# Attention of a hybrid layer: the score matmuls of two heads in two stretches per pair instead of four, the value matmuls in front of the first of them, 32 slots for every pair

## The chip, the core and the metric

The kernel runs on one core of a Trainium2 chip. Times are device microseconds of one execution. The kernel before was timed three times: 844.68, 844.88 and 845.14 us, median 844.88. The profile is of one further execution, which took 844.63 us; its span, from the first to the last instruction, is 842.8 us.

The engines are named as the profile names them: PE does the matmuls (PEld is its loading of the stationary operand), DVE is the vector engine, ACT the scalar engine, POOL the general engine, SP a queue that only issues transfers.

## What is computed

One decoder layer on 512 tokens of width 2048:

```
h = rms_norm(x);  z = h @ w_in                       # 2048 x 7168
a_val, a_glu, a_gate, q, k, v, b_gate = split(z)     # 1024 columns each
u = causal_depthwise_conv(a_val * sigmoid(a_glu))    # 31 taps
u = silu(layer_norm(u));  y_a = (u @ pw + b) * silu(a_gate)
q, k = rms_norm per head (16 heads of 64)
o = dilated_attention_mixture(q, k, v)               # causal, three window patterns
y_b = o * silu(b_gate)
out = x + concat(y_a, y_b) @ w_out
```

The three patterns of the attention are one softmax over all 512 keys, with the logarithm of the number of patterns that hold a key as a bias: a table (`tab`) that has -1e30 where none does.

## The kernel before, in words

**Units and slots.** All large matrix products are written as 76 units, each of 4 x 128 rows of a weight matrix by 512 columns. A unit is eight slots, and in a slot PE gets six matmuls of 512 columns (a product of two 16-bit halves, three matmuls each: `tri`, L360; the first 8 units use `exact_matmuls`, L713, in another number format). The loop at L810 counts the slots in `clock[0]`. Before a slot's matmuls it runs what a calendar holds for this slot (`after(n, fn)` puts `fn` n slots ahead), then the unit's own extras: in slot 0 of a unit ACT makes the high half `wh` of the next unit's weights (`split_hi`), in slot 2 DVE makes the low half `wl` (`split_lo`). PE needs both when the next unit begins. An instruction's place in the queue of its engine is thus set by the slot in which it was written; each engine works off its own queue in order and waits on semaphores for what other engines make.

**What fills DVE.** The depthwise convolution is a chain of DVE operations, written by a generator (`conv`, L476). `run_conv` (L702) takes one or more steps of it per slot, as long as the work given to DVE so far, counted in elements, is below 1200 per slot. After the last tap the generator writes the LayerNorm: sums over the eight channel tiles, a matmul with ones for the mean (L502), squares, a second set of matmuls for the variance (`token_rsqrt`, L342), the normalised tiles and `u16`, which the units named `pw` need from slot 448 on.

**Attention.** The heads go in eight pairs, four after the k projections of each half. `attention` (L647) starts pairs 32 slots apart in the first half and 40 in the second (`PERIOD`), always at the first slot of a unit. Within a pair (`two_heads`, L567) the plan at L636 says how many slots after the start each step is written:

- `scores(i)` for query tile i (128 queries, 128(i+1) keys): six matmuls with 64 rows of the array each, the two heads in the two row halves, then one DVE operation per head that adds `tab`, moves the scores to `sx` and takes the row maximum. Tiles 0, 1, 2, 3 stand at slots 0, 1, 4 and 5.
- `shift`, `exps` (ACT), `roots`, `high` and `low` (DVE; `high` on ACT in the first half) make normalised probabilities in two 16-bit halves, and `turn` transposes them by a DMA.
- `values`: 60 matmuls of 128 columns with 64 columns of the array each, the two heads in the two column halves, three slots before the next pair starts. `put` then multiplies with the gate on DVE, or copies on ACT where the gate isn't there yet.

PSUM has eight banks: four for the large products (`lin_ps`), three (`s_ps`) in turn for scores and small sums, one (`o_ps`) for `values`. A matmul that opens a bank waits until what the bank held has been read.

Of the kernel before, what the change touches and what calls it, by code (L numbers as in the profile page):

```python
# [10 lines left out]
F32 = mybir.dt.float32  # L11
# [5 lines left out]
OP = mybir.AluOpType  # L17
AX = mybir.AxisListType

P = 128  # L20
S = 512
# [10 lines left out]
LP = 4  # L32
WARM = 9
KU = 4
PERIOD = {0: 32, 1: 40}
START = 180
NORM_FROM = 37
PACE = 1200
# [37 lines left out]
def layer(ctx: ExitStack, tc: tile.TileContext, xt, w1, w2, w3, g_in, conv_w, conv_b,  # L76
          ln_g, ln_b, pw_b, q_g, k_g, table, out):
    nc = tc.nc
    A, G, T = nc.scalar, nc.gpsimd, nc.tensor
    V = Weighed(nc.vector)  # L80
    pool = lambda name, bufs, **kw: ctx.enter_context(tc.tile_pool(name=name, bufs=bufs, **kw))
    PS = bass.MemoryType.PSUM
# [6 lines left out]
    wide = pool("wide", 8)  # L89
    att = pool("att", 4)  # L90
    lin_ps = pool("lin_ps", LP, space=PS)
    s_ps = pool("s_ps", 7 - LP, space=PS)
    o_ps = pool("o_ps", 1, space=PS)
    ctx.enter_context(tc.manual_schedule())

    def slot(name):
# [13 lines left out]
    clock = [-1]  # L110

    def after(n, fn):

        calendar.setdefault(clock[0] + max(n, 1), []).append(fn)
# [361 lines left out]
    def conv():  # L476

        for i0 in range(0, 8, 2):
            while i0 + 1 not in u:
                yield 1  # L480
            for i in (i0, i0 + 1):
                cv[i] = slot("cv")
                A.activation(cv[i], u[i], AF.Identity, scale=cw[:, i, TAPS - 1:TAPS], bias=cb[:, i:i + 1])
            yield 2
            for j in range(TAPS - 2, -1, -1):
                d = TAPS - 1 - j
                for i in (i0, i0 + 1):
                    V.scalar_tensor_tensor(cv[i][:, d:], u[i][:, :S - d], cw[:, i, j:j + 1], cv[i][:, d:],
                                           op0=OP.mult, op1=OP.add)
                    yield 0  # L490
            u.pop(i0), u.pop(i0 + 1)

        wait[1] = True
        acc = temp("lnacc")
        V.tensor_add(acc, cv[0], cv[1])
        yield 0
        for i in range(2, 8):
            V.tensor_add(acc, acc, cv[i])
            yield 1
        yield 3  # L500
        mean = s_ps.tile([P, S], F32, name="ps_s")
        T.matmul(mean, ones, acc, start=True, stop=True)  # L502
        yield 1
        mean_sb = temp("mean")
        A.activation(mean_sb, mean, AF.Copy, scale=1.0 / C)
        yield 2
        acc2 = slot("lnacc2")
        squares = []
        for i in range(8):
            V.tensor_sub(cv[i], cv[i], mean_sb)  # L510
            if len(squares) > 1:
                V.tensor_add(acc2, acc2, squares.pop(0))
            if i == 0:
                A.activation(acc2, cv[i], AF.Square)
            else:
                squares.append(temp("lnsq"))
                A.activation(squares[-1], cv[i], AF.Square)
            yield 1 + i % 2
        while squares:
            yield 1  # L520
            V.tensor_add(acc2, acc2, squares.pop(0))
        yield 4
        c = small.tile([P, NT], F32, name="lncol")
        row = temp("lnrow")
        for _ in token_rsqrt(acc2, C, LN_EPS, c, row):
            yield 2
        yield 2
        for i in range(8 + 2):
            if i < 8:
                V.tensor_mul(cv[i], cv[i], row)  # L530
            if 1 <= i < 8 + 1:
                A.activation(cv[i - 1], cv[i - 1], AF.Silu, scale=lng[:, i - 1:i], bias=lnb[:, i - 1:i])
            yield 2
            if i >= 2:
                u16[i - 2] = split16(cv.pop(i - 2), scales["u"][0], "u16")
            yield 1
# [30 lines left out]
    def two_heads(pair):  # L567


        hf, p4 = divmod(pair, 4)  # L570
        halves = (slice(0, DH), slice(DH, P))
        st = [small.tile([P, 4 * NT], F32, name=f"st{a}") for a in range(2)]
        top, neg, total, root = ([t[:, j * NT:(j + 1) * NT] for t in st] for j in range(4))
        x = [att.tile([P, ALL], F32, name="sx", tag="att") for _ in range(2)]
        got = {}

        def scores(i):
            w = WIDTH[i]
            ps = [s_ps.tile([P, S], F32, name="ps_s") for _ in range(2)]
            for n, (q, k) in enumerate(((0, 0), (0, 1), (1, 0))):  # L580
                for a, rows in enumerate(halves):
                    T.matmul(ps[a][:, :w], qs[hf, q][rows, p4, i * P:w], ks[hf, k][rows, p4, :w], start=n == 0, stop=n == 2)  # L582
            for a in range(2):
                V.tensor_tensor_reduce(x[a][:, FROM[i]:FROM[i] + w], ps[a][:, :w], tab[:, S - w:], scale=1.0, scalar=-3e38,
                                       op0=OP.add, op1=OP.max, accum_out=top[a][:, i:i + 1])

        def shift(a):
            V.tensor_scalar(neg[a], top[a], nsc, None, op0=OP.mult)

        def exps(a, i):  # L590
            xi = x[a][:, FROM[i]:FROM[i] + WIDTH[i]]
            A.activation(xi, xi, AF.Exp, scale=sc, bias=neg[a][:, i:i + 1], accum_out=total[a][:, i:i + 1])  # L592

        def roots(a):
            V.tensor_scalar(total[a], total[a], 2.0 ** -P_SHIFT, None, op0=OP.mult)
            V.reciprocal(root[a], total[a])

        def high(a, i):
            if i == 0:
                got["p", a] = att.tile([P, 2 * ALL], F16, name="hl", tag="att")  # L600
            xi = x[a][:, FROM[i]:FROM[i] + WIDTH[i]]
            hi, r = got["p", a][:, FROM[i]:FROM[i] + WIDTH[i]], root[a][:, i:i + 1]
            if hf == 0:
                A.activation(hi, xi, AF.Copy, scale=r)
            else:
                V.tensor_scalar(hi, xi, r, None, op0=OP.mult)

        def low(a, i):
            hi, lo = (got["p", a][:, f + FROM[i]:f + FROM[i] + WIDTH[i]] for f in (0, ALL))
            V.scalar_tensor_tensor(lo, x[a][:, FROM[i]:FROM[i] + WIDTH[i]], root[a][:, i:i + 1], hi,  # L610
                                   op0=OP.mult, op1=OP.subtract)

        def turn(a):
            got["t", a] = att.tile([P, 2 * ALL // P, P], F16, name="pt", tag="att")
            nc.sync.dma_start(got["t", a], got["p", a], transpose=True)

        def values():
            got["o"] = po = o_ps.tile([P, S], F32, name="ps_o")
            for i in range(NT):
                for j in range(i + 1):  # L620
                    for n, (vp, pp) in enumerate(((0, 0), (1, 0), (0, 1))):
                        for a, rows in enumerate(halves):
                            T.matmul(po[rows, i * P:(i + 1) * P],  # L623
                                     vs[hf][j // 2][:, j % 2, 2 * p4 + a, vp * DH:(vp + 1) * DH],
                                     got["t", a][:, pp * (ALL // P) + FROM[i] // P + j, :],
                                     start=j == n == 0, stop=j == i and n == 2)

        def put():
            if pair in bg:
                ob[pair] = got["o"]  # L630
            else:
                ob[pair] = slot("opair")
                A.activation(ob[pair], got["o"], AF.Copy)
            gate_o(pair)

        plan = [(n, lambda i=i: scores(i)) for n, i in ((0, 0), (1, 1), (4, 2), (5, 3))]  # L636
        for a, e, h in ((0, 6, 10), (1, 14, 18)):
            plan += [(6 + a, lambda a=a: shift(a)), (h - 1, lambda a=a: roots(a)), (h + 6 - a, lambda a=a: turn(a))]
            for i in range(NT):
                plan += [(e, lambda a=a, i=i: exps(a, i)), (h + i // 2, lambda a=a, i=i: high(a, i)),  # L640
                         (h + 3 + i // 2, lambda a=a, i=i: low(a, i))]
        plan += [(PERIOD[hf] - 3, values), (PERIOD[hf] - 2, put)]
        return plan

    at_head = {}

    def attention(hf):  # L647
        start = -(-max(clock[0] + 28, max(at_head.values(), default=0) + PERIOD[0]) // 8) * 8
        for p4 in range(4):
            at_head[4 * hf + p4] = start + p4 * PERIOD[hf]  # L650

            def begin(pair=4 * hf + p4):
                for n, fn in two_heads(pair):
                    if n == 0:
                        fn()
                    else:
                        after(n, fn)
            after(at_head[4 * hf + p4] - clock[0], begin)


    def evac(group, m, ps):
# [228 lines left out]
```

## Time and profile before

| | |
|---|---|
| three timed runs, us | 844.68, 844.88, 845.14 |
| profiled execution, us | 844.63 |
| its span, us | 842.8 |
| PE busy, share of the span | 99% |
| DVE busy | 73% |
| ACT busy | 55% |
| POOL busy | 12% |
| granted TensorE clock | 1.00 |

The profile gives for each engine its instructions with start and length, and for each idle time what ended it. PE's matmuls overlap each other, so their lengths say less than the distance from one start to the next. The chain of waits lists the work that ended last, piece by piece, and so shows PE's stretches by such distances. Times in it are from the start of the span.

### The profile page before, as it was taken

Reading aid. Unit: us, or ns where it says so; the run is one execution under the profiler, and the core shown is the slowest. Engines: PE = TensorE matmul, PEld = TensorE weight load, DVE = VectorE, ACT = ScalarE, POOL = GpSimd, SP = SyncE. Lnnn points to the kernel's source line nnn. Section 1 sums busy time; section 2 is a strip of 40 time slices with the busy share of each in tenths; the row PEclk is TensorE's granted clock in tenths of the full one; section 3 lists DMA queues with packets and bytes.
Section 4 is the critical chain, followed back from the end, with each engine's and each line's share of the span. In section 5 each row is a group of like instructions: output and inputs, shape, how many; then the busy total and the mean of one; then the engine's idle time right before and its main releaser. Section 6 shows DMA issues by size and latency. Waiting matters only on the chain.

```text
span 842.8 us, 11262 instructions
## 1 busy us (share of the span) xinstructions
PE 838.2 (99%) x4394; PEld 413.3 (49%) x4394; DVE 611.5 (73%) x1023; ACT 462.6 (55%) x603; POOL 101.0 (12%) x131
## 2 busy tenths in 40 slices
PE   9999999999999999999999999999999999999998
PEld 6887644444444444444444444444444444444444
DVE  6658989888888978697878789286347697634343
ACT  7676644353655456676747558577486563333110
POOL 0001010101413101013031110001000000111100
PEclk9999999999999999999999999999999999999999
DMA  9922332222343525344555716326234476221022
GB/s 345 335 92 100 116 134 100 100 100 101 119 131 119 131 100 142 104 116 127 157 144 138 175 53 159 103 87 175 100 82 131 163 214 187 100 100 51 1 100 100
DMA packets 78948, 108.15 MB, mean 128 GB/s; under 512 B 62000, under 2 KB 62384, under 8 KB 69680
## 3 DMA queue, kind: packets, MB, share of 16 engines
q1 hardware_dynamic: 78608, 107.38, 41.5%
q8 instruction: 34, 0.56, 0.3%
q14 instruction: 18, 0.15, 0.1%
q10 hardware_dynamic: 288, 0.07, 0.0%
HBM read 88.56 MB, written 4.19 MB: 110 GB/s over the span
## 4 chain that ended last, share of the span: by engine, by line
PE 98%; DVE 1%; DMA 0%; issue 0%; ACT 0%; SPq 0%; DVEq 0%; ACTq 0%
PE ps_l L362 28%; PE ps_l L364 28%; PE ps_l L363 28%; PE ps_l L727 11%; PE ps_s L582 2%; PE ps_o L623 2%; DMA x<-xt_dram 0%; DVE wl L71 0%; PE ps_s L356 0%; PE ps_s L346 0%; DVE ya L71 0%; PE ps_s L502 0%; ACT hh L318 0%; DVE sx L71 0%; SPq L255 0%
## 5 line engine op out<-in xcount | busy, mean ns | idle before, releaser
L286 ACT ACTIVATE wh<-wf,ws 128x2048 f16<-128x2048 f32 x68 | 135.9, 1998 | 202.0 <-PE ps_l L363 195.8
L71 DVE SCALAR_TENSOR_TENSOR wl<-wf,ws,wh 128x2048 f16<-128x2048 f32 x68 | 159.7, 2348 | 37.1 <-ACT wh L286 36.8
L71 DVE SCALAR_TENSOR_TENSOR cv<-u,cw,cv 128x511 f32<-128x511 f32 (+14 forms) x240 | 161.6, 728 | 0.0
L362 PE MATMUL ps_l<-x,wh 128*128 128x512 f16 x384 | 145.7, 379 | 0.0
L362 PE MATMUL ps_l<-wh,x 128*128 128x512 f16 x384 | 145.7, 379 | 0.0
L364 PE MATMUL ps_l<-wh,x 128*128 128x512 f16 x384 | 145.5, 379 | 0.0
L363 PE MATMUL ps_l<-wl,x 128*128 128x512 f16 x384 | 145.5, 379 | 0.0
L364 PE MATMUL ps_l<-x,wl 128*128 128x512 f16 x384 | 145.5, 379 | 0.0
L363 PE MATMUL ps_l<-x,wh 128*128 128x512 f16 x384 | 145.5, 379 | 0.0
L182 ACT ACTIVATE junk<-wf 128x2048 bf16<-128x2048 f32 x68 | 129.1, 1898 | 3.5 <-DMA wf<-w_dram 3.4
L362 PEld LDWEIGHTS <-wh 128*128 128x128 f16 x708 | 69.2, 98 | 86.0 <-issue 5.5
L364 PEld LDWEIGHTS <-wl 128*128 128x128 f16 x708 | 69.2, 98 | 83.3 <-DVE wl L71 0.5
L363 PEld LDWEIGHTS <-wh 128*128 128x128 f16 x708 | 69.2, 98 | 77.8 <-issue 0.7
L363 PE MATMUL ps_l<-y,wh 128*128 128x512 f16 (+1 forms) x260 | 97.5, 376 | 0.0
L362 PE MATMUL ps_l<-y,wh 128*128 128x512 f16 (+1 forms) x260 | 97.5, 376 | 0.0
L364 PE MATMUL ps_l<-y,wl 128*128 128x512 f16 (+1 forms) x260 | 97.5, 376 | 0.0
L71 DVE SCALAR_TENSOR_TENSOR res<-ps_l,esc,res 128x512 f32<-128x512 f32 (+2 forms) x49 | 36.0, 737 | 53.7 <-PE ps_l L364 48.9
L196 POOL TENSOR_SCALAR ws<-ws 128x1 f32<-128x1 f32 x26 | 9.7, 372 | 520.8 <-DVE ws L71 520.8
L362 PEld LDWEIGHTS <-x 128*128 128x128 f16 x384 | 37.5, 98 | 47.1 <-issue 2.9
L364 PEld LDWEIGHTS <-x 128*128 128x128 f16 x384 | 37.5, 98 | 45.3
L363 PEld LDWEIGHTS <-x 128*128 128x128 f16 x384 | 37.5, 98 | 42.8
L592 ACT ACTIVATE sx<-sx,st,sc 128x128 f32<-128x128 f32 (+1 forms) x64 | 41.0, 641 | 28.1 <-DVE st L71 28.0
(179 smaller groups left out, 903.8 us busy)
## 6 DMA issues: line engine op xcount, KB each, us to landing
wf<-w_dram SPq DMA_DIRECT2D x72, 1024.0 KB, 4.9
x<-xt_dram SPq DMA_DIRECT2D x16, 256.0 KB, 6.6
res<-xt_dram SPq DMA_DIRECT2D x16, 256.0 KB, 5.4
out_dram<-res SPq DMA_DIRECT2D x15, 256.0 KB, 2.0
wf<-w_dram SPq DMA_DIRECT2D x7, 512.0 KB, 7.2
wf<-w_dram SPq DMA_DIRECT2D x2, 256.0 KB, 3.5
tab<-table_dram SPq DMA_DIRECT2D x1, 256.0 KB, 3.5
q<-qhl SPq DMA_TRANSPOSE x16, 3.2
```

The lines of the kernel that those rows point to most:

```text
L71: return getattr(self.engine, name)(out, src, *args, **kw)
L182: A.activation(junk[:, :n], src, AF.Square, scale=scale, accum_out=acc)
L196: G.tensor_scalar(scale, scale, 1e-30, 2.0 ** (-2 * top), op0=OP.max, op1=OP.mult)
L286: A.activation(parts[i][0], raw[i], AF.Copy, scale=wscale[units[i][3:]][0])
L362: T.matmul(ps, ah, bh, start=first, stop=False)
L363: T.matmul(ps, ah, bl, start=False, stop=False)
L364: T.matmul(ps, al, bh, start=False, stop=last)
L582: T.matmul(ps[a][:, :w], qs[hf, q][rows, p4, i * P:w], ks[hf, k][rows, p4, :w], start=n == 0, stop=n == 2)
L592: A.activation(xi, xi, AF.Exp, scale=sc, bias=neg[a][:, i:i + 1], accum_out=total[a][:, i:i + 1])
L623: T.matmul(po[rows, i * P:(i + 1) * P], vs[hf][j // 2][:, j % 2, 2 * p4 + a, vp * DH:(vp + 1) * DH], got["t", a][:, pp * (ALL // P) + FROM ...
L727: T.matmul(banks[group, m], wt[:, a, m * P:(m + 1) * P], xk[b], start=k == 0 and a == b == 0, stop=k == KC - 1 and a == 1)
```

## The change

Four things change. The scores of a pair are written in two stretches: tile 3 alone at the pair's first slot, then tiles 0, 2 and 1 three slots later, with tiles 0 and 2 of a head side by side in one bank. `values` and `put` of a pair are written where the next pair begins, directly in front of its first scores (for the last pair, one period after its start). The bank of `o_ps` joins `s_ps`, which has four banks now. Every pair has 32 slots and starts at the third slot of a unit; the steps between get other slots. In the LayerNorm two waits are added: the mean's matmul goes to the first slot of a unit, the variance's matmuls to the fifth slot of a unit in which no pair has begun within 8 slots.

```
-PERIOD = {0: 32, 1: 40}
+PERIOD = {0: 32, 1: 32}
+PHASE = 2
-    s_ps = pool("s_ps", 7 - LP, space=PS)
-    o_ps = pool("o_ps", 1, space=PS)
+    s_ps = pool("s_ps", 8 - LP, space=PS)
...
         yield 3
+        while clock[0] % 8:
+            yield 1
         mean = s_ps.tile([P, S], F32, name="ps_s")
...
         yield 4
+        while clock[0] % 8 != 4 or (clock[0] - at_pair[4]) % PERIOD[1] < 8:
+            yield 1
...
-        def scores(i):
-            w = WIDTH[i]
-            ps = [s_ps.tile([P, S], F32, name="ps_s") for _ in range(2)]
-            for n, (q, k) in enumerate(((0, 0), (0, 1), (1, 0))):
...
+        def scores(tiles):
+
+            ps = {}
+            for group in tiles:
+                for a in range(2):
+                    bank = s_ps.tile([P, S], F32, name="ps_s")
+                    for n, i in enumerate(group):
+                        f = sum(WIDTH[j] for j in group[:n])
+                        ps[i, a] = bank[:, f:f + WIDTH[i]]
+            order = [i for group in tiles for i in group]
+            for i in order:
+                w = WIDTH[i]
+                for n, (q, k) in enumerate(((0, 0), (0, 1), (1, 0))):
+                    for a, rows in enumerate(halves):
+                        T.matmul(ps[i, a], qs[hf, q][rows, p4, i * P:w], ks[hf, k][rows, p4, :w], start=n == 0, stop=n == 2)
+            for i in order:
+                w = WIDTH[i]
+                for a in range(2):
+                    V.tensor_tensor_reduce(x[a][:, FROM[i]:FROM[i] + w], ps[i, a], tab[:, S - w:], scale=1.0, scalar=-3e38,
+                                           op0=OP.add, op1=OP.max, accum_out=top[a][:, i:i + 1])
...
-            got["o"] = po = o_ps.tile([P, S], F32, name="ps_o")
+            got["o"] = po = s_ps.tile([P, S], F32, name="ps_o", tag="ps_s")
...
-        plan = [(n, lambda i=i: scores(i)) for n, i in ((0, 0), (1, 1), (4, 2), (5, 3))]
+        plan = [(0, lambda: scores(((3,),))), (3, lambda: scores(((0, 2), (1,))))]
...
-        plan += [(PERIOD[hf] - 3, values), (PERIOD[hf] - 2, put)]
...
+    def end_pair(pair):
+
+        for fn in to_come.pop(pair, ()):
+            fn()
...
-        start = -(-max(clock[0] + 28, max(at_head.values(), default=0) + PERIOD[0]) // 8) * 8
+        start = max(clock[0] + 28, max(at_pair.values(), default=0) + PERIOD[0])
+        start += (PHASE - start) % 8
...
-                for n, fn in two_heads(pair):
+                end_pair(pair - 1)
+                plan, values, put = two_heads(pair)
+                to_come[pair] = values, put
+                for n, fn in plan:
...
+                after(PERIOD[hf], lambda: end_pair(pair))
```

By the slot numbers that the loop counts, the eight pairs start at 224, 256, 288, 320, 352, 392, 432 and 472 before, and at 226, 258, ..., 450 (32 apart throughout) after the change; `values` of the last pair stand at 509 before and 482 after. The mean's matmul stands at 359 before and 360 after, the variance's at 380 and 396, the last `u16` tile at 415 and 431.

PE's queue, where the values of the first pair end. Before (`ps_o` is the values' bank, `pt` the transposed probabilities, `ps_l` a bank of the large products):

```order
L623 LDWEIGHTS v_2422
L623 MATMUL ps_o<-pt,v_2422 64x128
L362 LDWEIGHTS wh
L362 MATMUL ps_l<-x_978,wh 128x512
L363 LDWEIGHTS wh
L363 MATMUL ps_l<-x_978,wh 128x512
```

With the change (`ps_s` is a bank of scores):

```order
L638 LDWEIGHTS v_2419
L638 MATMUL ps_o<-pt,v_2419 64x128
L595 LDWEIGHTS q_1867
L595 MATMUL ps_s<-k_2189,q_1867 128x512
L595 LDWEIGHTS q_1867
L595 MATMUL ps_s<-k_2189,q_1867 128x512
L595 LDWEIGHTS q_1867
L595 MATMUL ps_s<-k_2191,q_1867 128x512
```

What followed the last value matmul was a matmul on the whole array; now it is the next pair's first score matmul on half of the rows.

DVE's queue at the second pair's scores. Before (`sx` takes the scores of one head, the rows `ISA st` with one column are the row maximum that goes with it, `cv` is the convolution):

```order
L71 ISA sx,st_2893<-ps_s,tab 128x256
L71 ISA st_2893 128x1
L71 ISA sx,st_2894<-ps_s,tab 128x256
L71 ISA st_2894 128x1
L71 SCALAR_TENSOR_TENSOR cv<-u,cw,cv 128x507
L71 SCALAR_TENSOR_TENSOR wl<-wf,ws,wh 128x2048
L71 ISA sx,st_2893<-ps_s,tab 128x384
L71 ISA st_2893 128x1
L71 ISA sx,st_2894<-ps_s,tab 128x384
L71 ISA st_2894 128x1
L71 ISA sx,st_2893<-ps_s,tab 128x512
```

With the change:

```order
L72 SCALAR_TENSOR_TENSOR gate<-ps_o,osc,gate 128x512
L72 ISA sx,st_2910<-ps_s,tab 128x512
L72 ISA st_2910 128x1
L72 ISA sx,st_2911<-ps_s,tab 128x512
L72 ISA st_2911 128x1
L72 SCALAR_TENSOR_TENSOR wl<-wf,ws,wh 128x2048
L72 ISA sx,st_2910<-ps_s,tab 128x128
L72 ISA st_2910 128x1
L72 ISA sx,st_2911<-ps_s,tab 128x128
L72 ISA st_2911 128x1
L72 ISA sx,st_2910<-ps_s,tab 128x384
```

The reads of tile 3's scores now stand in front of the low half `wl` of the next weights, and those of tiles 0, 2 and 1 behind it, one after the other; before, `wl` stood between the reads of tile 1 and those of tile 2.

DVE's queue in the units of slots 488 and 496, where `y` are the gated results made 16-bit for the last products (`ag` and `yas` for the convolution's, `yb1s` for the second half of the heads), up to the `wl` that the unit of slot 504 needs. Before:

```order
L71 SCALAR_TENSOR_TENSOR res<-ps_l,esc,res 128x512
L71 SCALAR_TENSOR_TENSOR hl<-sx,st_5738,hl 128x384
L71 SCALAR_TENSOR_TENSOR hl<-sx,st_5738,hl 128x512
L71 SCALAR_TENSOR_TENSOR y_6045<-ag_4590,yas,y_6045 128x512
L71 TENSOR_SCALAR y_6068<-gate,yas 128x512
L71 SCALAR_TENSOR_TENSOR res<-ps_l,esc,res 128x512
L71 SCALAR_TENSOR_TENSOR y_6068<-gate,yas,y_6068 128x512
L71 TENSOR_SCALAR y_6092<-gate,yas 128x512
L71 TENSOR_REDUCE ws<-ps_s 128x1
L71 SCALAR_TENSOR_TENSOR res<-ps_l,esc,res 128x512
L71 SCALAR_TENSOR_TENSOR y_6092<-gate,yas,y_6092 128x512
L71 SCALAR_TENSOR_TENSOR wl<-wf,ws,wh 128x2048
```

With the change:

```order
L72 SCALAR_TENSOR_TENSOR y_6108<-ag_4568,yas,y_6108 128x512
L72 SCALAR_TENSOR_TENSOR y_6110<-gate,yb1s,y_6110 128x512
L72 TENSOR_SCALAR y_6130<-gate,yas 128x512
L72 TENSOR_SCALAR y_6132<-gate,yb1s 128x512
L72 SCALAR_TENSOR_TENSOR res<-ps_l,esc,res 128x512
L72 SCALAR_TENSOR_TENSOR y_6130<-gate,yas,y_6130 128x512
L72 SCALAR_TENSOR_TENSOR y_6132<-gate,yb1s,y_6132 128x512
L72 TENSOR_SCALAR y_6157<-gate,yas 128x512
L72 TENSOR_REDUCE ws<-ps_s 128x1
L72 SCALAR_TENSOR_TENSOR res<-ps_l,esc,res 128x512
L72 SCALAR_TENSOR_TENSOR y_6157<-gate,yas,y_6157 128x512
L72 SCALAR_TENSOR_TENSOR wl<-wf,ws,wh 128x2048
```

The last pair's `hl` operations have left this stretch, and four of the `y` of `yb1s`, two operations each, have come into it, in front of the second `wl`.

## Rows read from the trace of the kernel before

**Rows 1.** The page: busy time of engines, granted clock in 40 slices.

```profile
PE 838.2 (99%) x4394; PEld 413.3 (49%) x4394; DVE 611.5 (73%) x1023; ACT 462.6 (55%) x603; POOL 101.0 (12%) x131
...
PEclk9999999999999999999999999999999999999999
```

**Rows 2.** Waits of PE: who waited for whom, total us, times, longest.

```profile
PE ps_s L582 <- DVE st L71: 0.3, 1, 0.3
PE ps_l L727 <- ACT hh L318: 0.2, 1, 0.2
```

**Rows 3.** The chain of waits, 32 slots without attention: start, us, piece.

```profile
118.02 0.24 PE ps_l L362
...
159.49 0.24 PE ps_l L362
```

**Rows 4.** The chain of waits over the second pair, up to the third.

```profile
349.17 0.27 PE ps_s L582 x6
349.45 0.32 PE ps_l L362
350.85 0.43 PE ps_s L582 x6
...
355.27 0.59 PE ps_s L582 x6
...
357.27 0.76 PE ps_s L582 x6
...
389.23 1.80 PE ps_o L623 x60
...
395.02 0.27 PE ps_s L582 x6
```

**Rows 5.** Waits of the weight loads (PEld) that nothing shown explains.

```profile
PEld L582 <- issue: 13.9, 33, 0.6
...
PEld L623 <- issue: 3.4, 8, 0.4
```

**Rows 6.** Timeline, the last pair's tile 3: start, us, engine, line, operation.

```profile
663.29 2.34 DVE L71 SCALAR_TENSOR_TENSOR wl<-wf,ws,wh 128x2048 f16<-128x2048 f32 x1
...
666.24 0.39 PE L582 MATMUL ps_s<-k,q 64*128 64x512 f16 x1
...
666.88 0.80 PE L582 MATMUL ps_s<-k,q 64*128 64x512 f16 x5 [0.25 <-DVE st L71]
```

**Rows 7.** Timeline, the begin of the unit of slot 456.

```profile
631.36 1.99 ACT L286 ACTIVATE wh<-wf,ws 128x2048 f16<-128x2048 f32 x1
...
633.39 2.35 DVE L71 SCALAR_TENSOR_TENSOR wl<-wf,ws,wh 128x2048 f16<-128x2048 f32 x1 [2.92 <-ACT wh L286]
...
635.37 0.38 PE L363 MATMUL ps_l<-u,wh 128*128 128x512 f16 x1
...
635.80 0.39 PE L364 MATMUL ps_l<-u,wl 128*128 128x512 f16 x1
```

**Rows 8.** Groups of DVE instructions by shape: busy us, mean ns, idle before.

```profile
L71 DVE SCALAR_TENSOR_TENSOR hl<-sx,st,hl 128x512 f16<-128x512 f32 x16 | 11.9, 745 | 0.0
...
L71 DVE CUSTOM_DVE_ANT_0 sx<-ps_s,tab 128x512 f32<-128x512 f32 x16 | 10.4, 689 | 5.7 <-PE ps_s L582 5.7
...
L71 DVE SCALAR_TENSOR_TENSOR gate<-ps_o,osc,gate 128x512 f32<-128x512 f32 x6 | 4.5, 747 | 2.5 <-PE ps_o L623 2.5
...
L71 DVE TENSOR_SCALAR hl<-sx,st 128x512 f16<-128x512 f32 x8 | 3.8, 480 | 0.0
...
L71 DVE SCALAR_TENSOR_TENSOR y<-gate,yb1s,y 128x512 f16<-128x512 f32 x4 | 3.0, 748 | 0.1
...
L71 DVE TENSOR_SCALAR y<-gate,yb1s 128x512 f16<-128x512 f32 x4 | 1.9, 478 | 0.0
```

**Rows 9.** Timeline, the begin of the unit of slot 504.

```profile
699.98 2.35 DVE L71 SCALAR_TENSOR_TENSOR wl<-wf,ws,wh 128x2048 f16<-128x2048 f32 x1
...
702.88 0.10 PEld L364 LDWEIGHTS <-wl 128*128 128x128 f16 x1
```

More of the change, by code (lines that the diff above doesn't have):

```diff
@@ L575, in two_heads @@
         got = {}
-        def scores(i):
-            w = WIDTH[i]
-            ps = [s_ps.tile([P, S], F32, name="ps_s") for _ in range(2)]
-            for n, (q, k) in enumerate(((0, 0), (0, 1), (1, 0))):
[L581 to L585, printed above, removed]
+        def scores(tiles):
[17 more added lines that the diff above has]
+                                           op0=OP.add, op1=OP.max, accum_out=top[a][:, i:i + 1])
         def shift(a):
@@ L634, in put @@
             gate_o(pair)
-        plan = [(n, lambda i=i: scores(i)) for n, i in ((0, 0), (1, 1), (4, 2), (5, 3))]
-        for a, e, h in ((0, 6, 10), (1, 14, 18)):
-            plan += [(6 + a, lambda a=a: shift(a)), (h - 1, lambda a=a: roots(a)), (h + 6 - a, lambda a=a: turn(a))]
+        plan = [(0, lambda: scores(((3,),))), (3, lambda: scores(((0, 2), (1,))))]
+        for a, e in ((0, 7), (1, 11)):
+            h = (13, 18)[a] if hf == 0 else e + 5
+            plan += [(6, lambda a=a: shift(a)), (e + 4, lambda a=a: roots(a)), (h + (6 if hf == 0 else 2), lambda a=a: turn(a))]
             for i in range(NT):
-                plan += [(e, lambda a=a, i=i: exps(a, i)), (h + i // 2, lambda a=a, i=i: high(a, i)),
-                         (h + 3 + i // 2, lambda a=a, i=i: low(a, i))]
-        plan += [(PERIOD[hf] - 3, values), (PERIOD[hf] - 2, put)]
-        return plan
-    at_head = {}
+                plan += [(e, lambda a=a, i=i: exps(a, i))]
+                if hf == 0:
+                    plan += [(h + i // 2, lambda a=a, i=i: high(a, i)), (h + 3 + i // 2, lambda a=a, i=i: low(a, i))]
+                else:
+                    plan += [(h, lambda a=a, i=i: high(a, i)), (h + 1, lambda a=a, i=i: low(a, i))]
+        return plan, values, put
+    at_pair, to_come = {}, {}
+    def end_pair(pair):
+        for fn in to_come.pop(pair, ()):
+            fn()
     def attention(hf):
-        start = -(-max(clock[0] + 28, max(at_head.values(), default=0) + PERIOD[0]) // 8) * 8
+        start = max(clock[0] + 28, max(at_pair.values(), default=0) + PERIOD[0])
+        start += (PHASE - start) % 8
         for p4 in range(4):
-            at_head[4 * hf + p4] = start + p4 * PERIOD[hf]
+            at_pair[4 * hf + p4] = start + p4 * PERIOD[hf]
             def begin(pair=4 * hf + p4):
-                for n, fn in two_heads(pair):
+                end_pair(pair - 1)
+                plan, values, put = two_heads(pair)
+                to_come[pair] = values, put
+                for n, fn in plan:
                     if n == 0:
@@ L657, in begin @@
                         after(n, fn)
-            after(at_head[4 * hf + p4] - clock[0], begin)
+                after(PERIOD[hf], lambda: end_pair(pair))
+            after(at_pair[4 * hf + p4] - clock[0], begin)
     def evac(group, m, ps):
```

## The prediction, made before the changed kernel ran

> **What bounds the kernel now.** I read the busy shares first: PE is busy 838.2 of 842.8 us at a granted clock of full speed in every slice, DVE and ACT far less [rows 1]. Then who makes PE wait: almost nobody, in all half a microsecond after the start [rows 2]. So PE's own stream is the time, and an edit gains only what it takes out of that stream, or loses what it makes PE wait. Last, the chain of waits, for what the stream consists of. Where no attention stands in it, 32 slots take 159.49 - 118.02 = 41.47 us [rows 3], which is 192 matmuls at 0.216. Over a pair of heads the same 32 slots take 395.02 - 349.17 = 45.85 us [rows 4]: a pair costs PE 4.38 us, eight pairs 35 us.
>
> What these 4.38 us are can be read from the pieces [rows 4]. The four stretches of scores take 0.27, 0.43, 0.59 and 0.76 us: 0.16 more for each 128 keys more. Three pairs of matmuls of 128 columns, the two heads side by side, are 384 columns, and 0.16 us for them is the 2.4 GHz of the granted clock. So tile 0 is 0.16 us of work and 0.11 that belong to the beginning of a stretch; the others have the same 0.11. Behind a stretch the first matmul on the whole array has 0.32 us in the chain and not 0.216: 0.104 for the end. The values take 1.80 us, and their end I take as the same 0.104. Check: 0.27 + 0.43 + 0.59 + 0.76 + 1.80 + 5 x 0.104 = 4.37, which is the pair's 4.38. So every stretch that works on half of the array costs 0.21 us beside its columns, and before there are five a pair, forty in all. The same is seen in the weight loads: before 33 stretches of score loads and 8 of value loads PEld stood idle about 0.42 us with nothing shown to wait for [rows 5]: the next weights, which are otherwise loaded while a matmul runs, are not loaded ahead across the border.
>
> The Trainium skill, TensorEngine Tiling (Array Packing), section Key Properties, says that a change of the tiling mode drains the engine, while another tile of the same mode doesn't. The 0.11 and 0.104 agree with it. By it the change from values (64 columns) to scores (64 rows) is one more drain and tiles of scores behind each other cost none, which gives 840.4; were that change free, it would be 839.6.
>
> **The change, part by part.**
>
> Stretches. Of the score stretches two are left a pair, and one of them has the values directly in front. Seven pairs have that; the first pair's tile 3 and the last pair's values stand alone. PE's new bill: eight stretches of tiles 0, 2 and 1 at 0.16 + 0.48 + 0.32 + 0.11 = 1.07, sum 8.6; eight times values at 1.80, sum 14.4; eight times tile 3 at 0.64 and a border of 0.11 in front, sum 6.0; ends: 8 + 7 + 2 = 17 at 0.104, sum 1.8. Together 30.7 against 8 x 4.37 = 35.0: **4.2 us less**. The one price here that no row shows is the border from values to scores inside a stretch. It can't well be more than what a return to the whole array between them would cost, 0.21, nor less than nothing: with 0.21 the gain is 3.5 us, with nothing 5.0. I take 0.11, since each border that the rows show costs about that.
>
> Stalls that go. At the last pair's tile 3 PE has 0.64 us from one matmul to the next, of which 0.21 are its 512 columns: it waits 0.43 us for a bank that DVE reads late, because `wl` stood in front of the read [rows 6]. With the change the reads of a stretch stand ahead of `wl`, or behind it by three slots. At the unit of slot 456 PE has 0.43 us between two matmuls and not 0.216: `wl` came late because `wh` did, behind exponentials of the seventh pair on ACT [rows 7]. This pair now starts 14 slots earlier and its exponentials are written at slots 425 and 429, before that crowd. **0.6 us less.**
>
> Banks. Values and tile 3 take three of the four banks at once and the second stretch all four, so it must find the gate's product and tile 3's two reads done: 0.75 for the gate, which DVE does while PE is at tile 3, then two reads of 0.69 [rows 8], about 1.5 us behind PE. The second stretch comes three slots, 3.9 us, later: 2.4 us to spare, with `wl` behind the reads in DVE's queue. I take nothing; what it costs if DVE is later is the second rival.
>
> Queues. Behind the gate's product, which waits for the values, DVE now has tile 3's reads and `wl` (2.35 us), and PE waits for that `wl` six slots on. From the border: 1.9 us of values, 0.75 of tile 3, 1.4 of reads, 2.35 of `wl` are some 6.5 us; PE needs 2.7 for the first stretch, 7.8 for six slots and 1.2 for the second, 11.7. So it has 5 us to spare. SP's transposes of the probabilities are written 14 and 18 slots (19 and 24 in the first half) behind the start, and their reader stands at 32, so SP may be late by eight slots. The sixteen fetches for the residual keep their slots. The LayerNorm's later matmuls cost PE what they did; its last tile is written at slot 431, and needed at 448.
>
> DVE towards the end. The second half's results are ready 28 slots sooner (values at 482, before at 509), so their four splits, 4 x (0.48 + 0.75) = 4.9 us of DVE [rows 8], move into slots 489 to 496, from behind. The last pair's eight `hl` operations of one head leave that place, the widest 0.48 and 0.75 [rows 8], eight of four widths some 3.5 us together. What stands next there is the `wl` for the unit of slot 504: before, it ended at 702.33 and PE's load took it at 702.88 [rows 9], 0.55 us to spare. The exchange takes about 1.4 us of it and the values at 482 give DVE about 1 us back, as PE is busy with them longer in that stretch. I count the rest as nothing left to spare. A second tight place is the unit of slot 472: the last pair's second `high` now stands in front of its `wl`. Both together I put at 0.3 us, an estimate from these terms; the bounds are nothing and the 2 to 3 us of a `wl` that is late by its whole length at one of them.
>
> **Sum.** -4.2 - 0.6 + 0.3 = **-4.5 us**. The profiled execution took 844.63 (842.8 of span and 1.8 around it, which the change doesn't touch), 0.25 below the median of the runs, so a like one should take 840.1 and the median **840.4**.
>
> **The rivals.**
>
> The border costs another thing than I think. If the 0.11 belongs to each tile of scores (its first weights, its banks) and not to the change of mode, only ends go: 40 - 17 = 23 at 0.104, 2.4 us, and with the stalls the gain is 2.7: 842.2. For it: every stretch before held one tile, so the rows can't tell the two apart. Against it: inside a tile the weights change at each matmul and cost nothing that shows. The second stretch of a pair would then take 1.29 us and not 1.07. Chance 0.10.
>
> The border inside a stretch costs nothing, and neither tight place does: 5.0 + 0.6, 839.3. For it: both modes use half of the array. Chance 0.13.
>
> `wl` late at several places: the convolution's and LayerNorm's work on DVE and ACT meets the pairs otherwise than before, in slots 360 to 384 and 464 to 504. Two or three stalls of about 1 us each leave a gain of 1.5 to 3: 842.6. For it: DVE is busy 73% of the span [rows 1], in bursts, and both stalls of before came of such bursts [rows 6, 7]. Against it: the convolution's steps are given to DVE only as far as its planned load allows. Chance 0.12.
>
> The other side: reading the banks becomes the bound. All 2560 columns of a pair's scores are now written in two bursts, and the second burst finds a free bank only if DVE has kept up. From 2.4 us of lag at the second stretch on, each further microsecond is a wait of PE, in every pair. To be slower by 0.2% the waits must eat 4.8 + 1.7 = 6.5 us, 0.8 a pair, so DVE must be 3.2 us behind at every pair: a `wl` in front of the reads would do that. The order has it behind them. 847. Chance 0.05.
>
> The Trainium skill, in the same page's section PSUM Bottleneck, warns of this: tiling speeds up the matmuls but not the reading of their results, which may become the bound. The wait of 0.43 us for a bank agrees that it can.
>
> **Chances and range.** Forecast as it stands 0.60 (839.8 to 841.2), the others as given: 0.10, 0.13, 0.12, 0.05. From the free border (839.3, less a little) to the late `wl` (842.6) holds over eight tenths: 838.9 to 842.9. A measurement of this kernel can tell about 0.2%, 1.7 us, from no change. Slower than that is the last rival, 0.05; within it falls the bad end of the late `wl`, and mixtures with the first rival, 0.06; faster 0.89.
>
> **What would show it.** In the chain of waits a pair should take 32 slots plus 3.83 us, 45.3 in all, in both halves; the stretch of tiles 0, 2, 1 should have 1.07 us and that of values and tile 3 2.55, of which tile 3 0.75. PEld's idle with nothing shown should come about 17 times behind whole-array matmuls, not 41. PE should wait for DVE less than 1 us in all. A second stretch of 1.29 us means the first rival; a pair's border that is absent the second; waits of PE's loads for `wl` the third; waits of `ps_s` matmuls for DVE at every pair the fourth. My sum is wrong if PE's stream shortens by less than 3 us with no waits to show for it.

## The result and the profile after

The changed kernel takes 840.02 us (median of 4 runs, 839.87 to 840.22); the kernel before, timed beside it, 844.96 (844.68 to 845.14). The ratio is 0.9942, with a 95% interval of 0.9925 to 0.9959: 4.9 us less, where 4.5 were forecast and the forecast time was 840.4.

The page of the changed kernel, its first part, answers to [rows 1]: busy us, share of the span, instructions of each engine.

```profile
PE 833.9 (99%) x4394; PEld 416.1 (50%) x4394; DVE 610.5 (73%) x1023; ACT 460.7 (55%) x601; POOL 90.9 (11%) x131
...
PEclk9999999999999999999999999999999999999999
```

PE has the same 4394 matmuls at the same granted clock and is still busy for 99% of a span that is 4.5 us shorter. So the gain is not work left out but time between matmuls.

The waits of PE in the changed kernel, all of them (who waited for whom: us in total, times, longest), answer to [rows 2]:

```profile
PE ps_s L138 <- POOL wz L135: 1.0, 1, 1.0
PE ps_l L755 <- ACT hh L318: 0.2, 1, 0.2
```

Both stand at the very beginning of the program, where the kernel before has the same two. The wait for DVE is gone, and none has come in its place. The waits of the weight loads with nothing shown to wait for answer to [rows 5]:

```profile
PEld L595 <- issue: 3.8, 9, 0.4
PEld L638 <- issue: 3.4, 8, 0.4
```

These are 17 places: the stretches on half of the array that begin behind a matmul on the whole array. Before there were 40 such stretches; of the 41 places in [rows 5] (33 and 8) one is the stall of [rows 6], in the middle of a stretch (timeline of the kernel before):

```profile
666.88 0.31 PEld L582 LDWEIGHTS <-q 64*128 64x128 f16 x4 [0.55 <-issue]
```

The mean stays at 0.42 us a place (13.9 / 33 before, 3.8 / 9 now): a border costs what it did, and there are fewer.

The chain of waits of the changed kernel (start, us, piece), the first pair's first stretch, then the second pair up to the third, answers to [rows 4]:

```profile
306.33 0.75 PE ps_s L595 x6
...
349.85 1.80 PE ps_o L638 x60
351.65 0.75 PE ps_s L595 x6
352.40 0.32 PE ps_l L362
...
356.39 1.09 PE ps_s L595 x18
357.48 0.32 PE ps_l L362
...
395.17 1.80 PE ps_o L638 x60
```

A pair is 395.17 - 349.85 = 45.32 us, before 45.85. The values run into tile 3 with no matmul on the whole array between, and tile 3 takes 0.75 us there, just what it takes alone at 306.33: its 0.64 of work and 0.11 for the border. The stretch of tiles 0, 2 and 1 takes 1.09.

For comparing whole programs one more pair of rows is useful: the chain's row of 42 matmuls in one of the first units, and the last instruction. Of the kernel before:

```profile
39.98 9.78 PE ps_l L727 x42
...
839.65 0.35 DVE res L71
```

and of the changed kernel:

```profile
40.39 9.78 PE ps_l L755 x42
...
835.11 0.35 DVE res L72
```

The same matmuls of the beginning start at 39.97 to 40.51 us in the twelve profiled executions of this study, in no order that an edit explains. All of this spread is there within the first 13 us; what makes it isn't shown. From there to the end the kernel before needs 799.67 us and the changed one 794.72: **4.95 us less**. I call this distance the run of a kernel; it is free of the beginning. There is one trace of each kernel, so how well this distance repeats was not measured. In the table below the medians lie 45.2 to 45.5 us above the runs, so the two measures agree to about 0.2 us from kernel to kernel.

### The profile page after: what moved, and what is told of

It reads as the page before. It is cut to its first block, busy times and chain, and to the rows that moved or that the text cites. A ratio compares the mean times of both kernels' runs of the same rounds, so it can differ in the third digit from the quotient of the medians.

```text
span 838.3 us, 11273 instructions
## 1 busy us (share of the span) xinstructions
PE 833.9 (99%) x4394; PEld 416.1 (50%) x4394; DVE 610.5 (73%) x1023; ACT 460.7 (55%) x601; POOL 90.9 (11%) x131
## 4 chain that ended last, share of the span: by engine, by line
PE 99%; DMA 0%; ACT 0%; SPq 0%; DVE 0%; issue 0%; ACTq 0%
PE ps_l L362 28%; PE ps_l L364 28%; PE ps_l L363 28%; PE ps_l L755 11%; PE ps_s L595 2%; PE ps_o L638 2%; DMA x<-xt_dram 0%; PE ps_s L356 0%; PE ps_s L346 0%; PE ps_s L504 0%; ACT hh L318 0%; SPq L255 0%; DVE res L72 0%; PE ps_s L194 0%; ACTq L318 0%
## 5 line engine op out<-in xcount | busy, mean ns | idle before, releaser
L364 PEld LDWEIGHTS <-x 128*128 128x128 f16 x384 | 37.6, 98 | 45.3
L755 PE MATMUL ps_l<-xr,wr 128*128 128x512 f32 x192 | 47.4, 395 | 0.0
```

The source lines that it names most:

```text
L364: T.matmul(ps, al, bh, start=False, stop=last)
L755: T.matmul(banks[group, m], wt[:, a, m * P:(m + 1) * P], xk[b], start=k == 0 and a == b == 0, stop=k == KC - 1 and a == 1)
```

## The experiments

Each kernel is compared with runs of the kernel before on the same chip (medians 845.14, 845.02 and 845.23 us). "Run" is the distance just defined.

| kernel | us, median | ratio, 95% interval | run, us |
|---|---|---|---|
| before | 844.96 | | 799.67 |
| changed | 840.02 | 0.9942 [0.9925, 0.9959] | 794.72 |
| stretches alone | 842.43 | 0.9966 [0.9952, 0.9979] | 797.14 |
| 32 slots alone | 844.34 | 0.9990 [0.9981, 0.9999] | 799.03 |
| values in front alone | 844.62 | 0.9995 [0.9986, 1.0004] | 799.17 |
| stretches and 32 slots | 840.71 | 0.9949 [0.9935, 0.9962] | 795.55 |
| changed, one stretch | 845.51 | 1.0004 [0.9995, 1.0013] | 800.23 |
| changed, second stretch one slot on | 840.24 | 0.9942 [0.9930, 0.9955] | 794.72 |
| changed, tile 1 apart | 841.75 | 0.9960 [0.9946, 0.9973] | 796.43 |
| changed, values apart | 840.82 | 0.9950 [0.9937, 0.9962] | 795.47 |
| changed, no LayerNorm waits | 842.41 | 0.9974 [0.9964, 0.9983] | 797.20 |
| changed, pairs at the first slot | 840.76 | 0.9949 [0.9935, 0.9962] | 795.38 |

### What a border costs: tile 1 apart, values apart

Tile 1 in a stretch of its own, one slot behind tiles 0 and 2:

```
-        plan = [(0, lambda: scores(((3,),))), (3, lambda: scores(((0, 2), (1,))))]
+        plan = [(0, lambda: scores(((3,),))), (3, lambda: scores(((0, 2),))), (4, lambda: scores(((1,),)))]
```

> The changed kernel with tile 1 in a stretch of its own, one slot behind tiles 0 and 2. Border theory: eight stretches more, 8 x 0.21 = 1.7 us more, 841.7 us; tile 1 takes 0.43 us as it did before and tiles 0 and 2 together 0.75. Rival (the gain is in the places, or in the shared bank): no change.

The chain of that kernel, its first pair:

```profile
311.01 0.76 PE ps_s L595 x12
...
313.17 0.43 PE ps_s L595 x6
```

Tile 1 behind the others in the same stretch costs 1.09 - 0.76 = 0.33 us, its columns alone; in a stretch of its own it costs 0.43 and, behind it, the 0.104 of the return. The run grows by 796.43 - 794.72 = 1.71 us, which is 8 x 0.214: eight borders both ways, at the price that the prediction read from the trace before. The first rival (the 0.11 belongs to each tile) asked for 0.43 in the shared stretch too, and so for 1.29 for the three tiles; they took 1.09, and it is out.

Values written two slots ahead of the next pair's tile 3, not directly in front:

```
-                after(PERIOD[hf], lambda: end_pair(pair))
+                after(PERIOD[hf] - 2, lambda: end_pair(pair))
```

> The changed kernel with the values two slots in front of the next pair's begin, so in a stretch of their own again. Border theory: seven ends at 0.104 come back, 0.7 us more, 840.7 us; tile 3 takes 0.75 us alone as it does behind the values. Rival (a border inside a stretch costs as much as a return): no change.

The chain of that kernel, from the second pair's values to its tile 3:

```profile
347.14 1.80 PE ps_o L638 x60
348.94 0.32 PE ps_l L362
...
351.63 0.75 PE ps_s L595 x6
```

Tile 3 takes 0.75 us alone, as it did behind the values, the matmul behind the values has 0.32 again, and the run grows by 0.75 us, seven times 0.107: the return to the whole array, once in each of seven pairs. So the border from values to scores inside a stretch costs the 0.11 of a beginning and spares the 0.104 of an end. This was the one price that no row before showed, with bounds of nothing and 0.21. The rival of a free border is out too. The Trainium skill, TensorEngine Tiling (Array Packing), section Key Properties, counts such a change as a change of mode, which drains; the 0.11 between values and tile 3 and the 0.33 of a third tile in the same mode agree with it.

### The parts of the change alone

The stretches, in the kernel before with all four banks in `s_ps` (`scores` as in the change; values, periods and starts as before):

```
-            got["o"] = po = o_ps.tile([P, S], F32, name="ps_o")
+            got["o"] = po = s_ps.tile([P, S], F32, name="ps_o", tag="ps_s")
...
-        plan = [(n, lambda i=i: scores(i)) for n, i in ((0, 0), (1, 1), (4, 2), (5, 3))]
+        plan = [(0, lambda: scores(((3,),))), (3, lambda: scores(((0, 2), (1,))))]
```

> The kernel before with the scores in two stretches (tile 3; then tiles 0, 2 and 1, three slots later) and four banks for scores and values; periods, starts and the values' own place stay as before. Border theory (each stretch on half of the array costs 0.21 us beside its columns): 40 stretches become 24, 16 x 0.214 = 3.4 us less, and the wait of 0.43 us at the last pair's tile 3 goes too, the 0.21 us at the unit of slot 456 stays: about 841.1 us. PE's stretch of tiles 0, 2 and 1 takes 1.07 to 1.10 us. Rival (the gain comes of the new periods and places, which take waits and crowding away, not of the borders): less than 1 us gained, 844 us or more.

Measured 842.43, 1.3 us more than I had said. Sixteen borders fewer are 3.4 us, and the 0.43 us wait for a bank is gone as well, but the run is only 2.53 shorter. The rest stands in its waits of PE:

```profile
PE ps_l L363 <- DVE wl L71: 1.3, 1, 1.3
```

and in the timeline of its unit of slot 504 (start, us, engine, line, operation):

```profile
698.57 2.35 DVE L71 SCALAR_TENSOR_TENSOR wl<-wf,ws,wh 128x2048 f16<-128x2048 f32 x1
...
699.31 0.38 PE L362 MATMUL ps_l<-y,wh 128*128 128x512 f16 x1
...
700.96 0.10 PEld L363 LDWEIGHTS <-wl 128*128 128x128 f16 x1 [1.77 <-DVE wl L71]
700.97 0.39 PE L363 MATMUL ps_l<-y,wl 128*128 128x512 f16 x1 [1.28 <-DVE wl L71]
```

From 699.31 to 700.97 are 1.66 us where 0.22 are work: 1.44 us lost, because PE arrived sooner than DVE could have `wl` ready. In the kernel before this `wl` had 0.55 us to spare [rows 9]. So the third rival (a late `wl`) did occur, only not in the changed kernel. -3.42 - 0.43 + 1.44 = -2.41, against -2.53 measured; the 0.12 between them I can't place.

The period alone:

```
-PERIOD = {0: 32, 1: 40}
+PERIOD = {0: 32, 1: 32}
```

> The kernel before with 32 slots for each pair of the second half too, nothing else. Border theory: still 40 stretches, so only waits can change, of which there are 0.64 us: 844.3 to 845.3 us, no change that a measurement can tell. Rival (periods and places give the gain): 843 us or less.

The run is 0.64 us shorter, and 0.64 is the sum of the two stalls of [rows 6] and [rows 7] (0.43 and 0.21). No wait of PE for DVE is left in its trace, while the 40 borders stand (32 places at L582, 8 at L623).

The values alone, written where the next pair begins, in front of its tile 0:

```
-        plan += [(PERIOD[hf] - 3, values), (PERIOD[hf] - 2, put)]
-        return plan
+        return plan, values, put
...
+                end_pair(pair - 1)
+                plan, values, put = two_heads(pair)
...
+                after(PERIOD[hf], lambda: end_pair(pair))
```

> The kernel before with the values of a pair directly in front of the next pair's first scores (tile 0), nothing else. Border theory: seven times an end and a beginning (0.21) become one border (0.11): 0.7 us less, 844.2 us, and the tile 0 stretch behind values takes 0.27 us as it did alone. Rival (a border between two modes that both use half of the array is free): the stretch of tile 0 behind values takes 0.16 us, 1.5 us less in all. Other rival (the change of mode inside a stretch costs a full return): no change.

The timed ratio can't tell this from no change. Tile 0 takes 0.27 us behind the values in the chain, as it did alone, so the border isn't free here either (0.16 would be). The run is 0.50 us shorter, where seven returns at 0.107 give 0.75. Six of the pairs' starts come nearer by 0.11 each, but the fifth pair's tile 3 loses 0.23 us: 1.05 us for six matmuls, 0.82 for the same tile elsewhere. Its loads go on at 494.96, just behind the read of a bank of tile 2, which ends at 494.89 (494.34 + 0.55).

```profile
494.34 0.55 DVE L71 CUSTOM_DVE_ANT_0 sx<-ps_s,tab 128x384 f32<-128x384 f32 x1
...
494.71 1.05 PE L582 MATMUL ps_s<-k,q 64*128 64x512 f16 x6
...
494.96 0.31 PEld L582 LDWEIGHTS <-q 64*128 64x128 f16 x4 [0.16 <-issue]
```

Two of the parts were smaller alone than their borders and stalls add up to, each because a new wait took some of it. To see whether the missing piece of the stretches belongs to them or to the place of the last pairs, I put 32 slots to them:

```
-PERIOD = {0: 32, 1: 40}
+PERIOD = {0: 32, 1: 32}
```

> Edit: the kernel before with two score stretches and four banks, as in the run of the stretches alone, and besides 32 slots for the pairs of the second half; values and pairs' starts at their old places. My theory: the stretches alone fell 1.1 us short of their sum because a `wl` of the unit of slot 504 came 1.44 us late and one of the unit of slot 456 by 0.21 us, both behind work of the last pairs; with 32 slots these pairs end earlier, both waits go, and the time is 842.43 - 1.65 = 840.8 (840.4 to 841.3). Rival: the shortfall belongs to the stretches themselves and the two edits only add up, 842.43 - 0.7 = 841.7 (841.4 to 842.3), or a new wait takes the old one's place, with a wait of PE over 1 us for DVE in the trace.

840.71, as my theory said, and not the 841.7 of edits that only add up. The run is 1.59 us shorter than with the stretches alone: 1.44 and 0.21 are 1.65. In the list of waits of that kernel PE waits for DVE nowhere:

```profile
PE ps_s L137 <- POOL wz L134: 1.0, 1, 1.0
PE ps_l L737 <- ACT hh L317: 0.3, 1, 0.3
```

The period is thus worth 0.64 us to the kernel before and 1.6 to one with merged stretches: most of what it does is to keep PE's gain from being given back.

### The banks: one stretch, and a second stretch one slot on

All four tiles in one stretch behind the values:

```
-        plan = [(0, lambda: scores(((3,),))), (3, lambda: scores(((0, 2), (1,))))]
+        plan = [(0, lambda: scores(((3,),))), (0, lambda: scores(((0, 2), (1,))))]
```

> The changed kernel with the second stretch directly behind the first, no slots between: values, tile 3, tiles 0, 2 and 1 in one. Border theory alone: eight borders of 0.21 less, 838.3 us. With the banks: four banks can't hold seven tiles; tile 0 of the second head waits for the gate's product (it ended 0.13 us behind the first stretch in the changed kernel's trace), tile 1 of the second head for the second read of tile 3 (1.34 us behind). PE waits some 0.6 to 0.8 us a pair and saves 0.21: 3 to 4.5 us more, 843 to 844.5 us, with PE waiting for DVE in nearly every pair. This shows what the evacuation rival would have cost, and where it decides.

Measured 845.51, 5.5 us above the changed kernel and 1 us above my range: a border less in each pair, and 0.69 us more for a pair (from one start of the values to the next on the timeline, 396.60 - 350.59 = 46.01). The timeline of this kernel at the second pair:

```profile
352.60 0.75 DVE L72 SCALAR_TENSOR_TENSOR gate<-ps_o,osc,gate 128x512 f32<-128x512 f32 x1 [3.45 <-PE ps_o L638]
353.27 0.68 DVE L72 CUSTOM_DVE_ANT_0 sx<-ps_s,tab 128x512 f32<-128x512 f32 x1
353.40 0.70 PEld L595 LDWEIGHTS <-q 64*128 64x128 f16 x12 [0.47 <-issue]
...
353.87 0.68 DVE L72 CUSTOM_DVE_ANT_0 sx<-ps_s,tab 128x512 f32<-128x512 f32 x1
...
354.62 0.48 PE L595 MATMUL ps_s<-k,q 64*128 64x256 f16 x5 [0.33 <-DVE st L72]
```

There are two waits, and the list of waits shows only the second, with 0.3 us eight times. First PE's loads stand still until 353.40, just behind the gate's product (352.60 + 0.75 = 353.35), which frees the bank of the values; then tile 1 stands until 354.62, behind the second read of tile 3 (353.87 + 0.68 = 354.55). This is the fourth rival's mechanism, made on purpose: the banks are wanted as fast as PE can write them, and all that the change gained is gone.

How near is the changed kernel to that? The second stretch one slot behind the first, not three:

```
-        plan = [(0, lambda: scores(((3,),))), (3, lambda: scores(((0, 2), (1,))))]
+        plan = [(0, lambda: scores(((3,),))), (1, lambda: scores(((0, 2), (1,))))]
```

> Edit: the changed kernel with the second stretch (tiles 0, 2, 1) one slot behind the first, not three. My theory: what a second stretch waits for is the reading of its banks, and only of the ones it takes back: its second bank is the one of the values, free when the gate's product ends 2.7 us behind the begin of the values, and tile 3's two banks, wanted by tile 1, are read 3.9 us behind it. One slot later the second stretch begins 2.55 + 0.10 + 1.30 = 3.95 us behind the begin of the values, and tile 1 another 0.75 later, so nothing is waited for; `wl` comes behind the reads some 10 us behind that begin and PE wants it at 11.7. Expected 840.0 to 840.8, with no pair's matmul waiting for DVE. Rival: the loss of 0.69 us a pair seen with both stretches in one comes from more than the banks (the amount of work DVE gets in one piece), and then most of it stays at a distance of one slot: 842 to 844, with a wait in most pairs.

840.24, and a run of 794.72, equal to the changed kernel's to a hundredth. So at one slot's distance the banks cost nothing, and the rival (the amount of work that DVE gets in one piece) is out: what is late in a single stretch is the reading of the banks. In the changed kernel the reads stand as follows (timeline, second pair):

```profile
351.78 0.75 DVE L72 SCALAR_TENSOR_TENSOR gate<-ps_o,osc,gate 128x512 f32<-128x512 f32 x1 [3.43 <-PE ps_o L638]
...
352.33 0.39 PE L362 MATMUL ps_l<-wh,x 128*128 128x512 f16 x1
...
352.45 0.68 DVE L72 CUSTOM_DVE_ANT_0 sx<-ps_s,tab 128x512 f32<-128x512 f32 x1
...
353.06 0.68 DVE L72 CUSTOM_DVE_ANT_0 sx<-ps_s,tab 128x512 f32<-128x512 f32 x1
...
353.67 2.35 DVE L72 SCALAR_TENSOR_TENSOR wl<-wf,ws,wh 128x2048 f16<-128x2048 f32 x1
...
356.32 1.16 PE L595 MATMUL ps_s<-k,q 64*128 64x128 f16 x18
```

The reads end at 353.74 (353.06 + 0.68), 1.41 us behind the first matmul on the whole array at 352.33 (I had said about 1.5), `wl` stands behind them in DVE's queue, and the second stretch begins 2.6 us later. The Trainium skill, TensorEngine Tiling (Array Packing), section PSUM Bottleneck, says that the reading of results can become the bound once tiling has made the matmuls faster; the 0.69 us a pair of the single stretch agree, and the 794.72 show how little distance undoes it.

### Where the rest of the work stands: LayerNorm's waits, pairs at the first slot

The two waits in the LayerNorm taken out of the changed kernel:

```
-        while clock[0] % 8:
-            yield 1
...
-        while clock[0] % 8 != 4 or (clock[0] - at_pair[4]) % PERIOD[1] < 8:
-            yield 1
```

> The changed kernel without the two waits that put the LayerNorm's matmuls in certain slots. My sum took the LayerNorm's moves as costing and giving nothing: no change, 840.0 within 0.5 us, PE's own waits staying near zero. Rival (the waits keep the LayerNorm's matmuls or its DVE work out of a pair's way): PE waits 1 us or more in the stretch of slots 355 to 400, 841 us or more.

My expectation failed and the rival was right: 842.41, a run longer by 2.48 us. Two rows of its waits and the matmul in question on the timeline:

```profile
PE ps_s L346 <- DVE lnacc L72: 1.3, 1, 1.3
...
PE ps_s L502 <- DVE st L72: 0.8, 1, 0.8
```

```profile
521.94 0.38 PE L364 MATMUL ps_l<-x,wl 128*128 128x512 f16 x1
...
522.10 1.47 DVE L72 TENSOR_TENSOR lnacc<-lnacc,lnsq 128x512 f32<-128x512 f32 x2
...
523.62 1.05 PE L346 MATMUL ps_s<-ones,lnacc 128*128 128x2 f32 x8 [1.30 <-DVE lnacc L72]
```

PE stands 1.46 us (1.68 from start to start, less 0.22) before the variance's matmuls, whose sum DVE has only just finished, and the mean's matmul, which then falls directly behind a second stretch, waits 0.8 us for a bank that this stretch holds. Waiting a few slots costs PE nothing, since it has other units to do; asking too early costs it the whole wait.

Pairs at the first slot of a unit:

```
-PHASE = 2
+PHASE = 0
```

> The changed kernel with the pairs starting at the first slot of a unit and not at the third, so that the low half of the next weights is written on DVE between the reads of the first stretch and those of the second. My account (2.4 us to spare for the banks, since what the second stretch needs is read ahead of it either way): the same borders, 840.0 within 0.7 us. Rival (the place relative to the weights' low half gives part of the gain): 1.7 us or more slower, with waits of PE for DVE.

840.76, by the median 0.06 more than I had allowed; the run grows by 0.66 us. It is one place: a matmul of the small sums, 0.03 us of work, waits for a bank and holds all of PE up, 0.87 us from start to start where 0.22 are work.

```profile
492.31 0.18 PE L194 MATMUL ps_s<-ysumb,ones 128*128 128x4 bf16 x1 [0.49 <-DVE st L72]
```

## Why the prediction was right, step by step

**The bound.** PE's own stream, 99% in both; every experiment moved the time by what it added to or took from that stream, or made it wait. Right.

**The price of a border, 0.11 in and 0.104 out.** Right, and shown by the two kernels that put borders back: 1.71 us for eight whole ones, 0.75 for seven returns. The pair's 45.32 us are the 45.3 forecast. The second stretch took 1.09 where I had 1.07, so its term was 0.02 a pair too small. The saving per pair is 45.85 - 45.32 = 0.53, which is five changes of mode at 0.107. Counted over the whole program there were 80 changes (in and out of 40 stretches) and there are 41 (17 in, 17 out and 7 from values to scores): 39 fewer, 4.17 us, and 4.2 were forecast. My "33 stretches of score loads" was a misreading that changed no term: there were 32, and the other place is the stall of [rows 6]. That both neighbouring modes use half of the array spares nothing at the border between them but the return.

**The stalls, -0.6.** Right: the kernel with 32 slots alone is shorter by 0.64. One thing I had put wrongly: I credited the bank stall to the stretches and the order of the reads, and either edit removes it, so it is not to be counted twice. The stall at slot 456 goes only with the period, as I had it.

**The tight places, +0.3.** This is the term that was mis-sized; it measured nothing. For the unit of slot 504 the timeline after, answering to [rows 9], has:

```profile
697.75 2.35 DVE L72 SCALAR_TENSOR_TENSOR wl<-wf,ws,wh 128x2048 f16<-128x2048 f32 x1
...
700.26 0.10 PEld L364 LDWEIGHTS <-wl 128*128 128x128 f16 x1
```

`wl` ends at 700.10 and PE's load of it is at 700.26, the first of the unit (132 matmuls of 22 slots behind the end of the values): 0.16 us to spare, before 0.55. My own terms, 0.55 - 1.4 + 1, leave 0.15; I rounded this to nothing and then gave it a price, and the last tenth held. Terms as rough as these can't tell 0.16 to spare from 0.16 too late, so that it held was partly luck. At the unit of slot 472 no wait shows either. Without the 0.3 the sum would have been -4.8, and 840.1. How near this was, the stretches alone show: the same `wl`, without the earlier pairs, was late by 1.44 us.

**The banks, nothing.** Right, and the margin was larger than I had worked out: I had asked that all reads be over before the second stretch. But that stretch opens a free bank first, then the values', and tile 3's two only for tile 1. Even one slot behind, with some 2.6 us less between, it does not wait.

**The LayerNorm, nothing.** Right for the change as a whole, but for a reason that I had not given: its waits are a part of the change without which new waits come (1.46 and 0.82 us from start to start, 2.28 of the 2.48 in the run). I had checked only what they would cost, not what would come without them. This is the weakest step of the prediction, though it didn't move its number.

**The sum.** 4.17 for the changes of mode and 0.64 for the stalls are 4.81; the run is 4.95 shorter, and 0.14 is left that I can't place. Of 4.95, 0.64 to 1.6 belong to the period (by what stands beside it), 0.83 to the values in front with the other starts, the slots of the steps between and the LayerNorm's waits (795.55 - 794.72; seven returns at 0.107 are 0.75 of it), and the rest to the stretches; the parts do not add up, because the stretches alone meet a late `wl` that the period removes.

## What to carry to other kernels

Where TensorE is the bound, count how often the stream changes between matmuls on the whole array and on halves of it, and price one change from the distances between starts: here 0.21 us there and back, which matmuls of the same mode put together save in full, and half of it where two modes follow each other directly. Merge until the banks are what is late, and leave about one burst of other matmuls between two merged stretches; here 1.3 us of them were enough and none cost all of the gain. And before counting the gain, look up what other engines must deliver sooner because TensorE now arrives earlier: a late operand at one place ate 1.4 of 3.8 us.

## What the runs showed that I had not expected

- A matmul with 0.03 us of work can cost 0.65: the small sums take their banks in turn with the scores, and PE, which works in order, stands behind them.
- The list of waits shows a wait smaller than it is. In the single stretch it names 0.3 us a pair for the second wait and nothing for the first. From 352.39 to 354.62 are 2.23 us, where about 1.3 are work (0.64 for tile 3, 0.16 and 0.48 for tiles 0 and 2), so both waits together cost some 0.9: the 0.69 that a pair got longer and the 0.21 of the border that it saved. A part is booked as the weight loads' own idle time (0.47 at the first). Distances between starts tell the whole.
- From the first units to the end, two profiled executions of kernels that differ only in the place of a stretch agree to 0.01 us (794.72 twice), while the beginning alone varies by 0.54 over the twelve. It is one pair of executions, and says no more.
